# All tiles at set offsets: matmul weights at odd, streamed operands at even multiples of 64 bytes of a partition

## The chip, the core and the metric

The kernel runs on one core of a Trainium2 chip. A core has TensorE (PE), which multiplies; VectorE (DVE), ScalarE (ACT) and GpSimd (POOL), which work on tiles; and SyncE (SP), whose queue issues the DMAs here. On-chip memory (SBUF) has 128 partitions; a tile takes the same range of bytes in each. A matmul on PE is two instructions: a weight load (LDWEIGHTS, shown as PEld), which reads the stationary operand, up to 128 columns, and a MATMUL, which streams the moving operand, up to 512 columns, past it. The weights of the next matmul are loaded while the present one streams, so both operands are read from SBUF at the same time. The metric is the device time of one execution in microseconds; lower is better.

## What is computed

```python
for i in range(2):                  # layer 0: pooling mixer, layer 1: attention
    sh1, sc1, g1, sh2, sc2, g2 = split(silu(c) @ ada_w[i] + ada_b[i], 6)
    a = rms_norm(h, norm_g[i, 0]) * (1 + sc1) + sh1
    h = h + g1 * (pool_mix(a) if i == 0 else attn_mix(a))
    m = rms_norm(h, norm_g[i, 1]) * (1 + sc2) + sh2
    h = h + g2 * (square(relu(m @ mlp_w1[i])) @ mlp_w2[i])   # 1024 -> 4096 -> 1024
return rms_norm(h, final_g)
```

There are 512 latent tokens and 256 context tokens of 1024 channels; the context goes through layer 0 and gives keys and values in layer 1. All of it is in float32.

## The kernel before

**How matmuls are written.** Channels lie on partitions, eight blocks of 128; tokens lie along the free axis. Nearly every operand x is held as two float32r halves, hi and lo with hi + lo = x (helper `hilo`, L91 on ACT and L92 on DVE), and a product is three matmuls: hi·hi, hi·lo, lo·hi. `pe.matmul(out, weights, moving)`: in the profile, `aux<-act,w` is a matmul into PSUM tile aux, with act streamed and w as weights.

**The stages, in order.** Start, pooling mixer and modulation vectors (to about 140 us; L192, L597, L641, L668, L764). The MLP of layer 0 (to about 630 us): 16 chunks of 256 hidden channels each; the first product is L376 in the first chunks and later L444, seven block products in place of eight (`m1_strassen`), with L464 for the context; the second product is L495 (`m2_chunk`), whose results L353 adds to `h_lat` and `h_ctx`. Attention (to about 890 us): L889 projects to keys, values and queries (`project`; here the activations `a_m_hi`, `a_m_lo`, `a_c` are the weights, and the weight tiles `w` are streamed), L967 and L968 are the scores (q as weights, k streamed), L988 transposes, L998 is probabilities by values (v as weights, `act` streamed), L1009 the output product. Then the MLP of layer 1, as in layer 0 but for 512 tokens alone.

**Where the tiles lie.** Pools take SBUF one behind the other in the order in which they are opened, and a pool's slots are its tile size times its number of buffers: `const`, `big` (`act`, `h_lat`, `h_ctx`, `m_hi`, `m_lo`), `wp` (four slots of 8192 bytes, tag `w`), `rp`, `sc`, `sm`, `mc` (five slots of 4096), `raws`, and then the pools of a stage, of which only one set is open at a time: `praws` and `pp` at first; `xs`, `op`, `pair` in the MLP of layer 0; `kvp` (k and v) in attention; `ss`, `fin`, `xs` in the MLP of layer 1. The tiles of `const` begin at a multiple of 128 bytes and take 2976 bytes, 23 times 128 and 32. The small tiles of `sm` take 2112 bytes, 16 times 128 and 64. Everything else that a matmul of float32r reads is a multiple of 128 bytes long. So, of the start of a tile's bytes modulo 128:

| tiles | before |
|---|---|
| `act`, `h_lat`, `h_ctx`, `m_hi`, `m_lo` (all `big`), `w`, `r`, `sc` | 32 |
| `mc` and all in its slots (`m_c`, `a_c`, q, o), `raw`, `xs`, `op`, `pair`, `ada`, k, v | 96 |
| `ident`, `ones` (in `const`) | 0 |

The order of the instructions is the tile framework's (by hand on PE, and for a stretch on DVE and ACT, in the pooling stage). In layer 1 the seven weight sums of a block product take five slots of `mc` and two halves of a tile `spare` in the slot of `h_ctx`:

```python
    def strassen1(m):
        def op():
            spare = new(big, [P, 2, 2, 512], F32R, "h_ctx")
            return lambda n: new(mc, [P, 2, 512], F32R, "mc") if n < 5 else spare[:, n - 5]
```

Of the kernel before, what the change touches and what calls it, by code (L numbers as in the profile page):

```python
# [8 lines left out]
F32 = mybir.dt.float32  # L9
F32R = mybir.dt.float32r  # L10
# [4 lines left out]
P = 128  # L15
D = 1024
KT = D // P
SEQ = 512
CTX = 256
# [4 lines left out]
HD = 128  # L24
# [23 lines left out]
def dit_block_kernel(ctx: ExitStack, tc: tile.TileContext, xT, cols, adab, adaw, w1, w2, wqkv, wo,  # L48
# [4 lines left out]
    def sb(stack, name, bufs):  # L53
        return stack.enter_context(tc.tile_pool(name=name, bufs=bufs))

    const = sb(ctx, "const", 1)
    big = sb(ctx, "big", 1)
    wp = sb(ctx, "wp", 4)
    rp = sb(ctx, "rp", 2)
    sc = sb(ctx, "sc", 4)  # L60
    sm = sb(ctx, "sm", 4)
    mc = sb(ctx, "mc", 5)
# [4 lines left out]
    scope = ExitStack()  # L67
# [2 lines left out]
    accp, rbp = (mc, "mc"), (rp, "r")  # L70

    acts2 = big.tile([P, 2, 4 * T], F32R, tag="act", name="act")
    uid = [0, 0]

    def new(p, shape, dt, tag, bufs=None):
        uid[0] += 1
        kw = {"bufs": bufs} if bufs else {}
        return p.tile(shape, dt, tag=tag, name=f"{tag}{uid[0]}", **kw)
# [17 lines left out]
    nc.sync.dma_start(ident, eye)  # L96
    pcol = const.tile([P, 8, KT], F32, tag="pcol", name="pcol")
    nc.sync.dma_start(pcol, cols)
    h_lat = big.tile([P, KT, SEQ], F32, tag="h_lat", name="h_lat")
    h_ctx = big.tile([P, KT, CTX], F32, tag="h_ctx", name="h_ctx")  # L100
    praw = (praws, [P, 1024], F32, "praw")
    ada_acc = ada_r = None
    edges = pp.tile([P, 4, 2, PAD], F32, tag="edges", name="edges")
# [13 lines left out]
    for u in range(0, 4, 2):  # L117
        pair = new(wp, [P, 2, 1024], F32, "w")
# [271 lines left out]
    def strassen_inputs(m, xs, tmp, cuts):  # L390


        def quarter(i, j):
            return [m[0][x][:, 4 * i : 4 * i + 4, 256 * j : 256 * j + 256] for x in range(2)]

        def total(dst, a, b, op):
            s, e = (new(tmp[0], [P, 4, 256], F32, tmp[1]) for _ in range(2))

            with tc.high_priority(offset=-BEHIND):
                for o, x in ((s, 0), (e, 1)):  # L400
                    dve.tensor_tensor(o, a[x].bitcast(F32), b[x].bitcast(F32), op=op)
                dve.tensor_tensor(s, s, e, op=ALU.add)
                hilo(dst[0], dst[1], s)

        b11, b12, b21, b22 = (quarter(i, j) for i in range(2) for j in range(2))
        b7, b6, b1 = ([t[:, x] for x in range(2)] for t in xs)
        sums = ((b7, b21, b22, ALU.add), (b6, b11, b12, ALU.add), (b1, b11, b22, ALU.add),
                (b12, b12, b22, ALU.subtract), (b21, b21, b11, ALU.subtract))

        def steps(todo):  # L410
            for x in todo:
                total(*x)
                yield
        return (b22, b12, b21, b11, b7, b6, b1), [steps(sums[i:j]) for i, j in zip((0,) + cuts, cuts + (5,))]
# [177 lines left out]
    for k in range(0, KT, 2):  # L592
# [10 lines left out]
        if k % 4 == 2:  # L603
            for i in range(6):
                x = (turned[0][:, i] if i < 4 else turned[1][:, i - 4])[:, k * P - 256 : k * P + 256]
# [239 lines left out]
    def strassen0(m):  # L845
        nonlocal scope, praw, ada_acc, ada_r
        scope.close()
        scope = ExitStack()
        xsp, opp, rawp = sb(scope, "xs", 1), sb(scope, "op", 3), sb(scope, "pair", 1)
        xs = [xsp.tile([P, 2, 4, 256], F32R, tag=f"xs{i}", name=f"xs0{i}") for i in range(3)]  # L850
        praw = (raws, [P, 1024], F32, "raw")
        ada_acc = new(mc, [P, 2, 512], F32, "mc")
        ada_r = [xsp.tile([P, 512], F32R, tag=f"ada{x}", name=f"ada{x}") for x in range(2)]

        def op():
            got = {}

            def tile_of(n):
                for key, pair in (("a", (1, 2)), ("b", (7, 8))):
                    if n in pair:  # L860
                        if key not in got:
                            got[key] = new(wp, [P, 2, 2, 512], F32R, "w")
                        return got[key][:, n - pair[0]]
                return new(opp, [P, 2, 512], F32R, "op")
            return tile_of
        return STRASSEN_FROM[0], strassen_inputs(m, xs, (opp, "op"), (0, 1, 3)), lambda: new(rawp, [P, 2, 1024], F32, "pair"), op

    norm = mlp(0, m, T, last, between=between0, strassen=strassen0, acts=[act0], ws=ws, ahead=lambda: kws.extend(load_w(wqkv[u]) for u in range(2)))
    am_ = lazy_m("a", True)


    scope.close()
    scope = ExitStack()
    kvp = sb(scope, "kvp", 1)
    accp = rbp = (mc, "mc")
    kk = kvp.tile([P, 2, NKV, T], F32R, tag="k", name="k")
    v = kvp.tile([P, 2, 6, NKV * HD], F32R, tag="v", name="v")

    tabs = big.tile([P, 4, 4, HD], F32, tag="h_ctx", name="tabs")
    scale = HD ** -0.5  # L880

    def project(ws, ps, width, tt):
# [228 lines left out]
    scope = ExitStack()  # L1111
# [3 lines left out]
    xsp = sb(scope, "xs", 1)  # L1115

    def strassen1(m):
        def op():
            spare = new(big, [P, 2, 2, 512], F32R, "h_ctx")
            return lambda n: new(mc, [P, 2, 512], F32R, "mc") if n < 5 else spare[:, n - 5]  # L1120

        xs = [xsp.tile([P, 2, 4, 256], F32R, tag=f"xs{i}", name=f"xs{i}") for i in range(3)]
        return STRASSEN_FROM[1], strassen_inputs(m, xs, (mc, "mc"), (1, 3)), lambda: new(fin, [P, 2, 1024], F32, "fin"), op
# [96 lines left out]
```

## Time and profile before

| | us |
|---|---|
| median of 3 runs | 1250.93 (1249.8 to 1253.14) |
| the profiled execution | 1251.34 |
| its span, first to last instruction | 1249.2 |
| PE busy | 1222.6, 7896 matmuls |
| weight loads busy | 1080.2 |
| DVE busy | 1016.9 |
| ACT busy | 589.5 |

The span is what the profile covers; 2.1 us of the execution's time lie around it. PE's busy time is the union of its records, and the record of a matmul is longer than its share of the stream, since one starts before the one ahead of it has ended: the distance from start to start has to be worked out.

### The profile page before, as it was taken

To read this page: it belongs to the slowest core of one execution; us is meant where nothing else is said; L and a number is where in the kernel's file an instruction comes from. 1 tells how busy PE (TensorE), PEld (TensorE's weight loads), DVE (VectorE), ACT (ScalarE), POOL (GpSimd) and SP (SyncE) were. 2 spreads that over 40 slices of the span, in tenths; PEclk is the share of its full clock that TensorE was granted. 3 is DMA by queue.
4 is the path that set the end of the run, shared out by engine and by line. 5 is a ranking of instruction groups with operands and counts; after the bars stand their busy time and mean duration, and the time that the engine had idled before them with its cause. 6 is when DMAs were issued, how large, how long until landed. Compare 5 with 4: busy or idle time off the path is not lost.

```text
span 1249.2 us, 20001 instructions
## 1 busy us (share of the span) xinstructions
PE 1222.6 (98%) x7896; PEld 1080.2 (86%) x7896; DVE 1016.9 (81%) x1723; ACT 589.5 (47%) x1055; POOL 143.1 (11%) x129
## 2 busy tenths in 40 slices
PE   7999999999999999999999999999999999999996
PEld 4767888899999999999988888888988999999996
DVE  6564998888989788866888387879899989898986
ACT  6554533444444444334455264554565454545443
POOL 0300000122131322231012001000000000000002
PEclk9999999999999999999999999999999999999998
DMA  9866424333433333321122020211223332323201
GB/s 351 329 238 218 136 85 139 114 119 119 153 111 133 129 123 120 129 68 34 46 82 85 17 85 18 68 34 67 102 86 101 111 109 92 111 94 110 75 28 68
DMA packets 41310, 138.64 MB, mean 111 GB/s; under 512 B 4736, under 2 KB 8064, under 8 KB 41088
## 3 DMA queue, kind: packets, MB, share of 16 engines
q1 hardware_dynamic: 41216, 137.36, 32.0%
q8 instruction: 62, 1.02, 0.3%
q14 instruction: 32, 0.26, 0.1%
HBM read 135.25 MB, written 2.10 MB: 110 GB/s over the span
## 4 chain that ended last, share of the span: by engine, by line
PE 63%; issue 27%; DVE 4%; ACT 2%; DMA 2%; POOL 1%; SPq 0%; POOLq 0%; DVEq 0%; ACTq 0%
PE aux L495 10%; PE mm L495 10%; PE aux L889 7%; PE mm L444 5%; PE aux L464 5%; PE mm L376 5%; PE aux L444 4%; PE aux L1009 3%; PE aux L998 3%; PE mm L967 2%; DMA raw<-in_dram 2%; PE aux L192 1%; PE mm L668 1%; PE mm L764 1%; PE aux L988 1%
## 5 line engine op out<-in xcount | busy, mean ns | idle before, releaser
L495 PE MATMUL aux<-act,w 128*128 128x512 f32 (+1 forms) x1224 | 238.8, 346 | 0.3 <-DVE h_lat L353 0.2
L495 PE MATMUL mm<-act,w 128*128 128x512 f32 (+1 forms) x1224 | 237.2, 345 | 0.9 <-DVE h_lat L353 0.9
L495 PEld LDWEIGHTS mm<-act,w 128*128 128x128 f32 x1224 | 194.9, 189 | 31.6 <-DVE h_lat L353 1.1
L495 PEld LDWEIGHTS aux<-act,w 128*128 128x128 f32 x1224 | 194.7, 189 | 29.6 <-DVE h_lat L353 0.7
L92 DVE TENSOR_TENSOR w<-raw,w 128x1024 fp32r<-128x1024 f32 x106 | 129.3, 1224 | 28.4 <-ACT w L91 28.3
L91 ACT ACTIVATE w<-raw 128x1024 fp32r<-128x1024 f32 x106 | 110.2, 1056 | 77.6 <-PE aux L495 40.7
L353 DVE SCALAR_TENSOR_TENSOR h_lat<-aux,mod,h_lat 128x512 f32<-128x512 f32 (+1 forms) x180 | 122.4, 686 | 16.9 <-PE aux L495 14.2
L433 POOL TENSOR_TENSOR sc<-pair 128x512 f32<-128x512 f32 x55 | 80.0, 1462 | 314.2 <-DMA raw<-in_dram 106.7
L353 DVE SCALAR_TENSOR_TENSOR h_lat<-mm,mod,h_lat 128x512 f32<-128x512 f32 (+1 forms) x140 | 97.7, 700 | 5.5 <-PE mm L495 4.6
L376 PE MATMUL mm<-m_m_hi,w 128*128 128x512 f32 (+1 forms) x320 | 92.9, 352 | 0.2 <-ACT m_m_hi L91 0.2
L889 PE MATMUL aux<-w,a_m_hi 128*128 128x256 f32 (+1 forms) x384 | 86.3, 320 | 0.0
L224 DVE SCALAR_TENSOR_TENSOR mc<-raw,s_f,mc 128x512 f32<-128x512 f32 x112 | 83.7, 765 | 2.1 <-DMA raw<-in_dram 1.3
L444 PE MATMUL mm<-m_m_hi,mc 128*128 128x256 f32 x384 | 69.8, 281 | 0.0
L889 PEld LDWEIGHTS aux<-w,a_m_hi 128*128 128x128 f32 x384 | 63.4, 190 | 5.0
L376 PEld LDWEIGHTS mm<-m_m_hi,w 128*128 128x128 f32 x320 | 56.3, 189 | 10.2 <-ACT r L384 0.8
L464 PE MATMUL aux<-m_c,w 128*128 128x256 f32 x528 | 61.6, 276 | 0.0
L889 PE MATMUL aux<-w,a_m_lo 128*128 128x256 f32 (+1 forms) x192 | 61.2, 319 | 0.0
L464 PEld LDWEIGHTS aux<-m_c,w 128*128 128x128 f32 x528 | 60.8, 188 | 0.0
L444 PEld LDWEIGHTS mm<-m_m_hi,mc 128*128 128x128 f32 x384 | 59.4, 188 | 0.5
L291 POOL TENSOR_TENSOR sm<-sm,neghalf 128x2 f32<-128x2 f32 (+1 forms) x9 | 6.6, 738 | 443.4 <-DVE sm L289 443.4
L376 PE MATMUL mm<-m_m_lo,w 128*128 128x512 f32 (+1 forms) x160 | 56.1, 351 | 0.7 <-DVE m_m_lo L92 0.7
L444 PE MATMUL mm<-m_m_lo,mc 128*128 128x256 f32 x192 | 53.9, 281 | 0.0
(260 smaller groups left out, 2453.9 us busy)
## 6 DMA issues: line engine op xcount, KB each, us to landing
raw<-in_dram SPq DMA_DIRECT2D x155, 512.0 KB, 3.8
praw<-in_dram SPq DMA_DIRECT2D x34, 512.0 KB, 7.7
fin<-in_dram SPq DMA_DIRECT2D x24, 512.0 KB, 4.4
pair<-in_dram SPq DMA_DIRECT2D x22, 512.0 KB, 4.6
block<-in_dram SPq DMA_DIRECT2D x8, 512.0 KB, 7.2
h_lat<-in_dram SPq DMA_DIRECT2D x4, 512.0 KB, 6.3
w<-in_dram SPq DMA_DIRECT2D x4, 512.0 KB, 10.7
out_dram<-fin SPq DMA_DIRECT2D x8, 256.0 KB, 2.5
```

The source lines that it names most:

```text
L91: act.activation(hi, src, AF.Copy)
L92: lo_eng.tensor_tensor(lo, src, hi.bitcast(F32), op=ALU.subtract)
L224: dve.scalar_tensor_tensor(acc[:, s], w, scal, acc[:, s], op0=ALU.mult, op1=ALU.add)
L353: dve.scalar_tensor_tensor(h, ps, gate[:, dt, s : s + 1], h, op0=ALU.mult, op1=ALU.add)
L376: pe.matmul(ps[:, c0 : c0 + cn], lhs, ms(m, ax, k, c0, cn), start=k + wx + ax == 0, stop=k == KT - 1 and wx == 1)
L433: eng.tensor_tensor(t, x, y, op=how)
L444: pe.matmul(places[n], w[:, wx, k * P : k * P + P], inputs[n][ax][:, k], start=k + wx + ax == 0, stop=k == 3 and wx == 1)
L464: pe.matmul(pc[:, t * 256 : t * 256 + 256], ws[k // 4][:, wx, k % 4 * P : k % 4 * P + P], ms(m, ax, k, SEQ, CTX), start=k + wx + ax == 0, ...
L495: pe.matmul(ps, lhs, a[:, t, ax, c0 : c0 + n], start=t + wx + ax == 0, stop=t == 1 and wx == 1)
L889: pe.matmul(ps, lhs, ws[u][:, wx, o : o + width], start=k + ax + wx == 0, stop=k == KT - 1 and ax == 1)
L998: pe.matmul(po, v[:, vx, k, g * HD : g * HD + HD], pT[:, px, k, j0:j1].rearrange("p j q -> p (j q)"), start=k + vx + px == 0, stop=k == 5 ...
L1009: pe.matmul(ps, ws[j][:, wx, dt * P : dt * P + P], o[ax][:, j, c0 : c0 + n], start=j + wx + ax == 0, stop=j == 1 and ax == 1)
```

## The change

No instruction is added or removed, and none of them changes its shape. Five tiles of spare words, which nothing reads or writes, are put between the pools (`skip`: 8 words of 4 bytes behind `const`, 16 words at the other places), `h_lat`, `h_ctx` and what follows in the slot of `h_ctx` move to a pool of their own, `odd`, and each tile of weight sums in layer 1 takes 1056 words of an `mc` slot and begins 16 words into it, so that all five slots of `mc` are 4224 bytes long.

```diff
     const = sb(ctx, "const", 1)
+    def skip(stack, n=16):
+        uid[2] += 1
+        sb(stack, f"skip{uid[2]}", 1).tile([P, n], F32, tag="skip", name=f"skip{uid[2]}")
+    uid = [0, 0, 0]
+    skip(ctx, 8)
+    odd = sb(ctx, "odd", 1)
+    skip(ctx)
     big = sb(ctx, "big", 1)
+    skip(ctx)
     wp = sb(ctx, "wp", 4)
...
-    h_lat = big.tile([P, KT, SEQ], F32, tag="h_lat", name="h_lat")
-    h_ctx = big.tile([P, KT, CTX], F32, tag="h_ctx", name="h_ctx")
+    h_lat = odd.tile([P, KT, SEQ], F32, tag="h_lat", name="h_lat")
+    h_ctx = odd.tile([P, KT, CTX], F32, tag="h_ctx", name="h_ctx")
...
-        xsp, opp, rawp = sb(scope, "xs", 1), sb(scope, "op", 3), sb(scope, "pair", 1)
+        xsp = sb(scope, "xs", 1)
+        skip(scope)
+        opp, rawp = sb(scope, "op", 3), sb(scope, "pair", 1)
...
+    skip(scope)
     kvp = sb(scope, "kvp", 1)
...
-    tabs = big.tile([P, 4, 4, HD], F32, tag="h_ctx", name="tabs")
+    tabs = odd.tile([P, 4, 4, HD], F32, tag="h_ctx", name="tabs")
...
-            spare = new(big, [P, 2, 2, 512], F32R, "h_ctx")
-            return lambda n: new(mc, [P, 2, 512], F32R, "mc") if n < 5 else spare[:, n - 5]
+            spare = new(odd, [P, 2, 2, 512], F32R, "h_ctx")
+            return lambda n: (new(mc, [P, 1056], F32R, "mc")[:, 16:1040].rearrange("p (x n) -> p x n", x=2) if n < 5
+                              else spare[:, n - 5])
```

By the same sums as before, modulo 128: `h_lat`, `h_ctx`, `w`, `r`, `sc`, `op`, k, v and the weight sums of layer 1 begin at 64; `act`, `m_hi`, `m_lo`, `mc` (with `m_c`, `a_c`, q and o), `raw`, `xs` and `ada` at 0. In the projections (L889) and the scores (L967, L968) the streamed tile is the odd one and the weights are the even one; in every other product of float32r but L232 (both at 0) it is the other way round.

More of the change, by code (lines that the diff above doesn't have):

```diff
@@ L72, in dit_block_kernel @@
     acts2 = big.tile([P, 2, 4 * T], F32R, tag="act", name="act")
-    uid = [0, 0]
     def new(p, shape, dt, tag, bufs=None):
```

## The prediction

> **What bounds the kernel now.** I read the page first, then busy time by stages of 50 us, who PE waits for, the groups of matmuls by form, and the timeline of PE alone.
>
> ```profile
> span 1249.2 us, 20001 instructions
> ...
> PE 1222.6 (98%) x7896; PEld 1080.2 (86%) x7896; DVE 1016.9 (81%) x1723; ACT 589.5 (47%) x1055; POOL 143.1 (11%) x129
> ...
> PEclk9999999999999999999999999999999999999998
> ```
>
> PE is busy nearly throughout, at full granted clock. Its waits for others are small, and the largest two are these, of the order of 9 us together, at the start and at the scores:
>
> ```profile
> PE mm L597 <- DMA h_lat<-in_dram: 6.8, 2, 6.3
> PE mm L967 <- ACT mc L91: 2.0, 4, 0.5
> ```
>
> So the time is set by how fast PE takes matmul after matmul. The share of busy time doesn't tell that, since records overlap. The timeline does, where one form follows itself: the run's length less one record, divided by the count less one, is the distance from start to start.
>
> ```profile
> 251.32 4.47 PE L444 MATMUL aux<-xs,op 128*128 128x256 f32 x36
> 255.64 5.60 PE L464 MATMUL aux<-m_c,w 128*128 128x256 f32 x48
> ```
>
> Both runs have 256 columns and 128 columns of weights. With the mean record of the first table below, L464 goes at (5600 - 276) / 47 = 113.3 ns and L444 at (4470 - 283) / 35 = 119.6 ns. Nothing is waited for in either. What differs is the place in SBUF: in L464 the streamed `m_c` begins at 96 modulo 128 bytes and the weights at 32; in L444 `xs` and `op` both begin at 96. In both rows record less distance is 163 ns, so the mean record of a form tells its distance: 276 stands for 113.3, 283 for 120. For 512 columns the same holds:
>
> ```profile
> 701.70 10.89 PE aux L889 x48
> ```
>
> Here 48 matmuls of 512 columns start within 10.89 us, 226.9 ns each, twice 113.3 within the reading; a record of 226.7 + 163 = 389.7 is the undisturbed one. Now the twenty largest forms (line, tiles out<-streamed,weights, count, busy us, mean record in ns):
>
> ```profile
> L495 PE MATMUL mm<-act,w 128*128 128x512 f32 x696 | 206.8, 393 | 0.0
> L495 PE MATMUL aux<-act,w 128*128 128x512 f32 x696 | 204.1, 394 | 0.3 <-DVE h_lat L353 0.2
> L495 PE MATMUL mm<-act,w 128*128 128x256 f32 x528 | 119.8, 281 | 0.9 <-DVE h_lat L353 0.9
> L495 PE MATMUL aux<-act,w 128*128 128x256 f32 x528 | 114.3, 281 | 0.0
> L444 PE MATMUL mm<-m_m_hi,mc 128*128 128x256 f32 x384 | 69.8, 281 | 0.0
> L376 PE MATMUL mm<-m_m_hi,w 128*128 128x512 f32 x192 | 68.5, 396 | 0.0
> L464 PE MATMUL aux<-m_c,w 128*128 128x256 f32 x528 | 61.6, 276 | 0.0
> L444 PE MATMUL mm<-m_m_lo,mc 128*128 128x256 f32 x192 | 53.9, 281 | 0.0
> L376 PE MATMUL mm<-m_c,w 128*128 128x256 f32 x192 | 53.4, 278 | 0.0
> L444 PE MATMUL aux<-xs,op 128*128 128x256 f32 x396 | 50.0, 283 | 0.0
> L889 PE MATMUL aux<-w,a_m_hi 128*128 128x256 f32 x256 | 46.5, 283 | 0.0
> L889 PE MATMUL aux<-w,a_m_hi 128*128 128x512 f32 x128 | 39.8, 392 | 0.0
> L376 PE MATMUL mm<-m_m_lo,w 128*128 128x512 f32 x96 | 37.8, 393 | 0.0
> L967 PE MATMUL mm<-k,mc 128*128 128x512 f32 x96 | 37.2, 420 | 2.2 <-ACT mc L91 2.0
> L889 PE MATMUL aux<-w,a_m_lo 128*128 128x256 f32 x128 | 36.2, 283 | 0.0
> L444 PE MATMUL aux<-xs,h_ctx 128*128 128x256 f32 x288 | 35.9, 279 | 0.0
> L1009 PE MATMUL aux<-mc,w 128*128 128x512 f32 x144 | 35.2, 392 | 0.0
> L444 PE MATMUL mm<-m_m_hi,op 128*128 128x256 f32 x176 | 34.7, 281 | 0.0
> L444 PE MATMUL mm<-m_m_hi,w 128*128 128x256 f32 x176 | 33.6, 283 | 0.0
> L998 PE MATMUL aux<-act,v 128*128 128x512 f32 x126 | 30.6, 395 | 0.0
> ```
>
> No form of 256 columns is under 276 and none of 512 is under 390. The distances look like steps: 113.3, 120 and 226.7 ns are 17, 18 and 34 times 6.67 ns. If a step is the time of 16 columns, which are 64 bytes of float32, then a matmul beside a weight load loses between nothing and one line of 64 bytes. I read this as two readers meeting in one half of the memory, the half being chosen by the 64-byte bit of the address. It is a reading, and the rivals start from other ones.
>
> **The change, part by part.** It leaves the instructions, their order and their shapes alone. The skipped words cost bytes and no time, as nothing touches them. What moves is the offset at which PE's two operands begin, and that of every other engine and DMA.
>
> *The loss that is there to win.* For the rows of 256 columns, count times (record - 276): L495 2 x 528 x 5 = 5.28 us; L444 with `mc` 384 x 5 + 192 x 5 = 2.88; with `xs,op` 396 x 7 = 2.77; with `xs,h_ctx` 288 x 3 = 0.86; `m_hi,op` 176 x 5 = 0.88; `m_hi,w` 176 x 7 = 1.23; L376 `m_c` 192 x 2 = 0.38; L889 384 x 7 = 2.69. Sum 16.97 us. For 512, against 389.7: L495 696 x 3.3 + 696 x 4.3 = 5.29; L376 192 x 6.3 + 96 x 3.3 = 1.53; L889 128 x 2.3 = 0.29; L1009 144 x 2.3 = 0.33; L998 126 x 5.3 = 0.67. Sum 8.11 us. L967 is left out, as its 420 ns hold waits. Together 25.1 us in 5946 matmuls, 2% of the time, and this is all that the meeting of readers costs in these rows.
>
> *What the change does to it.* After it, weights lie at 64 and streamed tiles at 0 in all these rows but L889. That is the layout of L464 (streamed 96, weights 32) moved on by 32 bytes. If the layout gives what it gives in L464, 528 times over, 25.1 - 2.98 (L889) = 22.1 us go. The other end: two other rows have L464's offsets already, L376 with `m_c` (278) and L444 with `xs,h_ctx` (279), and over the three the loss is (192 x 2 + 288 x 3) / 1008 = 1.24 ns; L1009, with the same offsets and 512 columns, loses 2.3. With these, the 2380 matmuls of 256 columns that now have another layout go from 13.04 to 2.95 us, and the 1806 of 512 (L495, L376, L998) from 7.49 to 4.15: 13.4 us are won. I take 22.1, since L464 is the largest of these rows and the only one that never leaves 276, and since starts at 64 and 0 split no 64-byte line between two halves, as starts at 32 and 96 do.
>
> *L889 and the scores* stand the other way round, streamed at 64 and weights at 0. The nearest row is L444 with `mc` (streamed 32, weights 96): 281. L889 would go from 283 to 281 in 384 matmuls, 0.8 us at best; at 512 columns the nearest is L998 (streamed 32, weights 96),
>
> ```profile
> 732.07 4.36 PE L998 MATMUL aux<-act,v 128*128 128x512 f32 x18
> ```
>
> (4360 - 395) / 17 = 233.2 ns (35 steps), 6.5 over 226.7, where L889 now loses 2.3: 128 x 4.2 = 0.5 us lost. I put the two at nothing.
>
> *The other engines.* DVE, ACT, POOL and the DMAs do the same work at new offsets. No row shows them at 0 or 64, so I bound them by what would reach PE. DVE is closest to it (stretch and length, then busy us with the count for PE, weight loads, DVE, ACT and POOL):
>
> ```profile
> 150.00:200.00 50.00, 50.00 (x289) 43.34 (x288) 48.67 (x65) 18.78 (x23) 1.30 (x1) 1.00 0.29 95
> ...
> 900.00:950.00 50.00, 50.00 (x297) 44.41 (x296) 47.38 (x62) 25.48 (x39) 0.70 (x1) 1.00 0.32 98
> 950.00:1000.00 50.00, 50.00 (x281) 43.85 (x281) 47.74 (x63) 25.24 (x36) 0.00 (x0) 1.00 0.34 114
> ```
>
> DVE's slack is 1.3 us of 50 in the first of these and 2.3 to 2.6 in the others. A PE that is 22.1 / 1249 = 1.8% faster asks for 0.9 us per 50, so DVE stays behind PE, just. Were DVE's operations 3% slower at the new offsets, these stages would need 50.1, 48.8 and 49.2 us where PE needs 49.1, and lose 1.0, 0 and 0.1 us: I take nothing, and up to 2 us as the worse end. A faster DMA or DVE wins nothing, as only the 9 us of waits could shrink. The wider slots of `mc` hold the same tiles and set free no one earlier or later.
>
> *Sum.* 1251.3 us of the profiled execution less 22.1 is 1229.2. That execution lies 0.4 above the median of the runs, so against the median 1229.
>
> **Rivals.** *The grid itself matters (B).* Even the best rows may pay for starting at 32 or 96: 113.3 ns are 17 steps, where 256 columns of 4 bytes have 16 lines of 64, and 226.7 are 34, where 512 columns have 32. Started on a line, a matmul could take fewer. PE can go faster than 113.3:
>
> ```profile
> 736.26 0.82 PE L988 MATMUL aux<-ident,r 128*128 128x128 f32 x6
> ```
>
> ```profile
> L988 PE MATMUL aux<-ident,r 128*128 128x128 f32 x192 | 26.4, 273 | 0.4 <-DVE r L978 0.4
> ```
>
> Six transposes, (820 - 273) / 5 = 109 ns apart (0.82 us less one mean record of 273, over five). At 109 and 218 the rows gain a further 3772 x 4.3 + 2174 x 8.7 = 35.1 us and L889 its 3: 1251.3 - 25.1 - 35.1 = 1191. The far end is set by the weight load, whose record grows from 108 to 188 ns between 32 and 128 columns:
>
> ```profile
> L464 PEld LDWEIGHTS aux<-m_c,w 128*128 128x128 f32 x528 | 60.8, 188 | 0.0
> ...
> L192 PEld LDWEIGHTS aux<-praw,s_w 128*32 128x32 f32 x136 | 4.1, 108 | 10.9 <-issue 7.2 <-DMA praw<-in_dram 3.5
> ```
>
> That is 0.83 ns a column, 106.7 for 128: 3772 x 6.6 + 2174 x 13.3 = 53.8 more than the 25.1, and 1172. Against it: a whole line lost at 256 and two at 512 look like a rate, which may belong to float32r and not to the start; and at 5% DVE's slack above would be used up. [...]
>
> *The offsets don't decide (C).* `xs,h_ctx` has L464's offsets and runs at 279, L495, with both operands at 32, is at 281 and not at 283, and the 48 matmuls of L889 above, both at 32 too, lose nothing. Then the loss comes from how the two streams fall into step, which a shift doesn't mend: what L464 wins or loses, L495 gives back, and the time stays within 0.3%, 1247.6 to 1255.1, about what a measurement of this kernel can tell from no change. [...]
>
> *Aligned lines meet (D, slower).* Both streams now change lines at the same instants, and while one line of weights is read, two of the moving operand pass, one in each half. So wherever the weights begin, each load could meet the stream and cost one line, 6.7 ns. That decides if even one such meeting per load is unavoidable on the grid, which the split lines of now sometimes escape. All rows at 283 and 396.4: 3772 x 7 - 16.97 = 9.4 us, and 2174 x 6.7 - 8.11 = 6.5 us; 1251.3 + 15.9 = 1267. For it: `mc` and v as weights at 96, the half that is nominally odd, are at 281 and 395, worse than `w` at 32. Against it: no row but `xs,op`, `m_hi,w` and L889, all with equal offsets, is at 283.
>
> **How the numbers follow.** The forecast (A, 1229, between 1229 and 1238) has 0.42, B 0.25, C 0.17, D 0.16. The range goes from 1177, which takes in B but for its far end, to 1254, which takes in C; D is left out, and the rest of B. Faster by over 0.3% are A and B, 0.67; within 0.3% is C, 0.17; slower is D, 0.16.
>
> **What would show it.** The counts must stay: 7896 matmuls and as many loads. By A, L464 stays at 276, and `xs,op`, `m_hi,w`, L495 and L444 with `mc` come down to 276 and 390; L889 stays at about 283. By B, L464 itself and the rows of 512 fall under 276 and 389. By D, L464 rises to 283. By C, rows move both ways and the sum doesn't. In the stages from 900 to 1000 us DVE should come to 97%; if PE then shows waits for DVE there, the gain is cut by them. The forecast is wrong if L495, which has 10.6 of the 25.1 us, keeps 281 and 393.

## The result, and the profile after

The changed kernel takes 1254.94 us (median of 12 executions, 1252.67 to 1257.23), the kernel before 1251.77. The ratio is 1.0024, with a 95% interval of 1.0015 to 1.0033: slower by 0.24%, or 3.2 us. The profiled execution took 1254.41 us.

The page of the kernel after, its span and the busy time by engine:

```profile
span 1252.3 us, 20001 instructions
...
PE 1225.7 (98%) x7896; PEld 1077.9 (86%) x7896; DVE 1019.5 (81%) x1723; ACT 588.2 (47%) x1055; POOL 140.8 (11%) x129
...
PEclk9999999999999999999999999999999999999999
```

As many instructions as before, the same clock, and 3.1 us more span, all of it in PE's busy time. Who PE waits for (us in total, times, longest), in the kernel after:

```profile
PE mm L607 <- DMA h_lat<-in_dram: 6.8, 2, 6.4
PE mm L980 <- ACT mc L101: 2.0, 4, 0.5
```

The same 6.8 and 2.0 us. So neither an engine nor a transfer came between: the matmuls themselves follow each other more slowly. The groups of matmuls by form show which (L505 was L495, L454 was L444, L474 L464, L386 L376, L902 L889):

```profile
L505 PE MATMUL mm<-act,w 128*128 128x512 f32 x696 | 209.3, 396 | 0.0
L505 PE MATMUL aux<-act,w 128*128 128x512 f32 x696 | 207.0, 398 | 0.2
L505 PE MATMUL mm<-act,w 128*128 128x256 f32 x528 | 119.2, 280 | 1.1 <-DVE h_lat L363 1.1
...
L454 PE MATMUL mm<-m_m_hi,mc 128*128 128x256 f32 x384 | 69.7, 280 | 0.0
L386 PE MATMUL mm<-m_m_hi,w 128*128 128x512 f32 x192 | 69.1, 398 | 0.0
L474 PE MATMUL aux<-m_c,w 128*128 128x256 f32 x528 | 63.9, 280 | 0.0
...
L902 PE MATMUL aux<-w,a_m_hi 128*128 128x256 f32 x256 | 45.5, 280 | 0.0
...
L454 PE MATMUL aux<-xs,h_ctx 128*128 128x256 f32 x288 | 34.6, 276 | 0.0
```

The rows of 512 columns rose: those of L505 from 393 and 394 to 396 and 398 (696 x 3 + 696 x 4 = 4.9 us), that of L386 from 396 to 398. L474 rose from 276 to 280 (528 x 4 = 2.1 us), `m_c` in L386 from 278 to 281. Most of the other rows of 256 columns fell, by 1 to 4 ns, and `xs,mc` from 283 to 276. The second product of layer 1 shows the rise at 512 columns best. PE's timeline, first one row of before, then four of after (start, length in us):

```profile
984.45 2.91 PE L495 MATMUL mm<-act,w 128*128 128x512 f32 x12
```

```profile
252.63 4.40 PE L454 MATMUL aux<-xs,op 128*128 128x256 f32 x36
256.87 5.77 PE L474 MATMUL aux<-m_c,w 128*128 128x256 f32 x48
...
984.97 2.88 PE L454 MATMUL aux<-xs,h_ctx 128*128 128x256 f32 x24
987.69 2.96 PE L505 MATMUL mm<-act,w 128*128 128x512 f32 x12
```

Before: (2910 - 393) / 11 = 228.8 ns; after: (2960 - 396) / 11 = 233.1. And L474 goes at (5770 - 280) / 47 = 116.8 instead of 113.3, while `xs,op` goes at 117.7 instead of 119.6 and `xs,h_ctx` at 113.2.

In what follows a **distance in bytes** is the start of the weights less the start of the streamed operand beside which they are loaded, modulo 256. The change moved it so: `act,w` and `m,w` from 0 to 64, `m_c,w` from 192 to 64 and 192 in turn (the `mc` slots of 4224 bytes alternate by 128), `xs,op` from 0 to 64, `m,mc` from 64 to 64 and 192, L889's `w,a_m` from 0 to 192; `xs,h_ctx` stayed at 192 and `act,v` at 64.

**Lost time** below is the sum, over all matmuls of float32r that another one follows, of the time from start to start less 113.3 ns (256 columns) or 226.7 (512). Single steps that are over 25 ns too long hold waits and stops and are left out. It is 29.3 us before and 31.9 after, 2.6 of the 3.1 us by which the span grew.

### The profile page after: what moved, and what is told of

It is laid out like the page before. It is cut to its first block, busy times and chain, and to the rows that moved or that the text cites. A ratio compares the mean times of both kernels' runs of the same rounds, so it can differ in the third digit from the quotient of the medians.

```text
span 1252.3 us, 20001 instructions
## 1 busy us (share of the span) xinstructions
PE 1225.7 (98%) x7896; PEld 1077.9 (86%) x7896; DVE 1019.5 (81%) x1723; ACT 588.2 (47%) x1055; POOL 140.8 (11%) x129
## 4 chain that ended last, share of the span: by engine, by line
PE 63%; issue 27%; DMA 3%; DVE 3%; ACT 2%; POOL 1%; SPq 0%; POOLq 0%; DVEq 0%; ACTq 0%
PE aux L505 10%; PE mm L505 10%; PE aux L902 8%; PE aux L474 5%; PE mm L454 5%; PE mm L386 5%; PE aux L454 4%; PE aux L1022 3%; PE aux L1011 3%; PE mm L980 2%; DMA raw<-in_dram 2%; PE mm L774 1%; PE aux L1001 1%; PE mm L678 1%; PE aux L202 1%
## 5 line engine op out<-in xcount | busy, mean ns | idle before, releaser
L505 PE MATMUL aux<-act,w 128*128 128x512 f32 (+1 forms) x1224 | 240.7, 347 | 0.2
L505 PE MATMUL mm<-act,w 128*128 128x512 f32 (+1 forms) x1224 | 238.7, 346 | 1.1 <-DVE h_lat L363 1.1
L505 PEld LDWEIGHTS mm<-act,w 128*128 128x128 f32 x1224 | 194.3, 188 | 33.8 <-DVE h_lat L363 1.3
L505 PEld LDWEIGHTS aux<-act,w 128*128 128x128 f32 x1224 | 194.1, 188 | 32.1 <-DVE h_lat L363 0.6
L386 PE MATMUL mm<-m_m_hi,w 128*128 128x512 f32 (+1 forms) x320 | 93.2, 353 | 0.3 <-ACT m_m_hi L101 0.2
L902 PE MATMUL aux<-w,a_m_hi 128*128 128x256 f32 (+1 forms) x384 | 85.5, 318 | 0.0
L454 PE MATMUL mm<-m_m_hi,mc 128*128 128x256 f32 x384 | 69.7, 280 | 0.0
L902 PEld LDWEIGHTS aux<-w,a_m_hi 128*128 128x128 f32 x384 | 62.7, 188 | 5.1
L386 PEld LDWEIGHTS mm<-m_m_hi,w 128*128 128x128 f32 x320 | 56.0, 188 | 11.0 <-ACT r L394 0.8
L474 PE MATMUL aux<-m_c,w 128*128 128x256 f32 x528 | 63.9, 280 | 0.0
L474 PEld LDWEIGHTS aux<-m_c,w 128*128 128x128 f32 x528 | 62.9, 188 | 0.0
L902 PE MATMUL aux<-w,a_m_lo 128*128 128x256 f32 (+1 forms) x192 | 60.8, 317 | 0.0
L454 PEld LDWEIGHTS mm<-m_m_hi,mc 128*128 128x128 f32 x384 | 59.6, 188 | 0.5
L386 PE MATMUL mm<-m_m_lo,w 128*128 128x512 f32 (+1 forms) x160 | 56.2, 352 | 0.7 <-DVE m_m_lo L102 0.7
L386 PE MATMUL mm<-m_c,w 128*128 128x256 f32 x192 | 53.9, 281 | 0.0
```

The source lines that it names most:

```text
L386: pe.matmul(ps[:, c0 : c0 + cn], lhs, ms(m, ax, k, c0, cn), start=k + wx + ax == 0, stop=k == KT - 1 and wx == 1)
L454: pe.matmul(places[n], w[:, wx, k * P : k * P + P], inputs[n][ax][:, k], start=k + wx + ax == 0, stop=k == 3 and wx == 1)
L474: pe.matmul(pc[:, t * 256 : t * 256 + 256], ws[k // 4][:, wx, k % 4 * P : k % 4 * P + P], ms(m, ax, k, SEQ, CTX), start=k + wx + ax == 0, ...
L505: pe.matmul(ps, lhs, a[:, t, ax, c0 : c0 + n], start=t + wx + ax == 0, stop=t == 1 and wx == 1)
L902: pe.matmul(ps, lhs, ws[u][:, wx, o : o + width], start=k + ax + wx == 0, stop=k == KT - 1 and ax == 1)
```

## The experiments

The theories at first were these. 1: the relative place of weights and streamed operand decides, and the width of the matmul decides which place is good. 2: the 64-byte grid itself costs or gains. 3: the offsets decide nothing, and how two streams fall into step is chance.

**Matmuls alone.** A kernel that leaves out all the rest streams tiles `ma` to `md`, starting at 0, 32, 64 and 96 modulo 128, past weights `wa` to `wd` that start alike. By the sizes of the tiles, pairs of the same letter are at distance 0 modulo 256 too, `ma,wc` and `mb,wd` at 64.

> The matmuls alone: runs of 48 float32r matmuls of zeros, in the order hi-hi, hi-lo, lo-hi, with the streamed tile starting at 0, 32, 64 or 96 bytes modulo 128 (ma, mb, mc, md) and the weights likewise (wa, wb, wc, wd), 512 and 256 columns wide, each once behind a pause of transposes and once chained; the rest of the computation is left out and the output is zero. Theory 1 (only whether both begin in the same 64-byte half counts, and the width decides which is better): at 512 columns the pairs aa, ab, ba, bb and cc, cd, dc, dd go at 226.7 ns and the others at 233 to 235; at 256 the same pairs go at 120 and the others at 117.7 or 113.3; starts at 0 and 32 do not differ. Theory 2 (starts on the 64-byte grid cost, split lines escape): bb and bd at 512 and db, bd at 256 are faster than aa, ac, ca by 4 ns or more. Theory 3 (chance of the phase, nothing in the offsets): the same pair gives different distances behind the pause and chained, and no pair is better on average by over 1 ns.

Groups by form, with one run of 48 matmuls in a row:

```profile
L87 PE MATMUL chained<-ma,wc 128*128 128x512 f32 x48 | 11.4, 394 | 0.0
...
L87 PE MATMUL chained<-ma,wb 128*128 128x512 f32 x48 | 11.4, 395 | 0.0
...
L87 PE MATMUL chained<-ma,wa 128*128 128x512 f32 x48 | 11.1, 390 | 0.0
...
L87 PE MATMUL chained<-mc,wc 128*128 128x512 f32 x48 | 11.1, 389 | 0.0
...
L87 PE MATMUL chained<-mb,wb 128*128 128x256 f32 x48 | 5.9, 282 | 0.0
...
L87 PE MATMUL chained<-mb,wd 128*128 128x256 f32 x48 | 5.6, 276 | 0.0
```

Equal starts are the best for 512 columns, on the grid of 32 or on that of 64, and among the worst for 256, where 64 apart gives 276. Theory 2 has nothing here. Theory 1 has its first miss: `ma,wb`, with both starts in the same half, was to go at 226.7 ns and goes at 233 by the starts in the trace. Of theory 3, one part holds at 256 columns: by the starts, `mc,wa` goes at 117.8 ns behind a pause and at 113.3 chained. The other part falls: at 512 columns equal letters are the best both ways, by 2 ns and more (but for the very first run, whose records have 442 ns on average).

**The grid in the whole kernel**, from both sides: the changed kernel without its first eight spare words (weights at 32, streamed operands at 96), and the kernel before with eight words behind `const`.

```diff
-    skip(ctx, 8)
```

> The changed kernel without its first 8 spare words: weights at 32 and streamed tiles at 96 everywhere, so the halves stay different and the grid of the kernel before comes back; this is what L464 had before, for all products. Theory 1 (halves): as the changed kernel, 1254.9 us, the 512-column rows of the second product at 396 to 398 ns. Theory 2 (grid): the loss of the 512-column rows is gone, 390 ns, and with the 256-column rows at 276 to 280 the time is 1229 to 1247. Theory 3: within 0.1% of either kernel.

```diff
     const = sb(ctx, "const", 1)
+    sb(ctx, "skip", 1).tile([P, 8], F32, tag="skip", name="skip")
```

> The kernel before with 8 spare words behind the constants and nothing else: every tile moves by 32 bytes, onto the 64-byte grid, and all pairs keep their relation. Theory 1 (halves): as the kernel before, 1251.8 us, the 512-column rows of the second product at 393 and those of layer 1 at 390. Theory 2 (grid): 1255 or more, the 512-column rows at 396 to 398. Theory 3: within 0.1% of either kernel.

The first took 1254.34 us, ratio 1.0021 (1.0011 to 1.0031), the second 1251.41, ratio 1.0000 (0.9990 to 1.0009), both against 1251.48. Off the grid the changed kernel stays slow, on it the old one stays as it was. What does it is the place of the tiles to each other.

**`act` moved to an odd place in the changed kernel**, so that it lies with the weights modulo 128; modulo 256 it is then 128 away from them.

```diff
-    acts2 = big.tile([P, 2, 4 * T], F32R, tag="act", name="act")
+    acts2 = odd.tile([P, 2, 4 * T], F32R, tag="act", name="act")
```

> The changed kernel with the act tile moved into the pool of the odd tiles, so that the second product of both MLPs has streamed tile and weights in the same half again, and all else stays as changed. Theory 1 (halves by width): its 512-column rows come back to 393 and 390 ns (4.4 us), the 256-column matmuls between 512-column ones win 1.2 us, the ones behind one another lose 2.1 us: 1254.9 - 3.5 = 1251.4. Theory 2 (grid): no change from 1254.9. Theory 3: within 0.1% of either.

1250.03 us, ratio 0.9984 (0.9976 to 0.9993): within 1.4 us of the total that was expected, but not by its rows:

```profile
L505 PE MATMUL mm<-act,w 128*128 128x512 f32 x696 | 208.7, 394 | 0.1
L505 PE MATMUL aux<-act,w 128*128 128x512 f32 x696 | 206.3, 396 | 0.3
L505 PE MATMUL mm<-act,w 128*128 128x256 f32 x528 | 120.6, 283 | 0.8 <-DVE h_lat L363 0.8
...
L454 PE MATMUL mm<-m_m_hi,mc 128*128 128x256 f32 x384 | 68.0, 277 | 0.0
```

The rows of 512 columns win back about half of their loss and not all of it (the runs of twelve in layer 1 still go at 233.7 ns by their starts), 256 columns are worse, and the gain came in the first product, which the edit doesn't touch (280 to 277). Theory 1 had the modulus wrong.

**The modulus, in steps of 32 bytes.** Again matmuls alone: one stream `m`, weights `wa` to `wq` at 0 to 512 bytes behind it, runs of 36; then other widths, and a first matmul of another width ahead.

> The matmuls alone again, with zeros, the rest of the computation left out and the output zero: one streamed tile, and weights at 0, 32, ... 512 bytes behind it modulo 512 (wa, wb, ... wq), 36 matmuls each, behind a pause and chained, at 512 and 256 columns; then 512 and 256 in turn, other widths, and a first matmul of another width ahead of the run. The kernel with act among the odd tiles had streams and weights both at 64 modulo 128 and yet lost 6.5 ns at 512 columns; its distance was 128. Theory 1 (distance of weights behind the stream modulo 256 decides, by width): 512 columns: 226.7 ns at 0 and 256 and 512, 228.9 at 192 and 448, 233 at 64, 128 and 320; 256 columns: 120 at 0, 128, 256, 113.3 or 117.8 at 64 and 192. Theory 2 (no memory of the distance beyond the half, the loss is inherited from the products around): 128 behaves as 0, 226.7 at 512 columns and 120 at 256. Which of 113.3 and 117.8 comes depends on the width of the first matmul if the phase of entry decides.

PE's timeline, for 0 (`wa`), 64 (`wc`), 128 (`we`), 192 (`wg`) and 256 bytes (`wi`), first with 256 columns, then with 512:

```profile
258.13 4.48 PE L87 MATMUL chained<-m,wa 128*128 128x256 f32 x36
270.89 4.43 PE L87 MATMUL chained<-m,we 128*128 128x256 f32 x36
283.70 4.47 PE L87 MATMUL chained<-m,wi 128*128 128x256 f32 x36
300.80 4.26 PE L87 MATMUL chained<-m,wc 128*128 128x256 f32 x36
313.47 4.25 PE L87 MATMUL chained<-m,wg 128*128 128x256 f32 x36
330.33 8.36 PE L87 MATMUL chained<-m,wa 128*128 128x512 f32 x36
355.17 8.53 PE L87 MATMUL chained<-m,we 128*128 128x512 f32 x36
380.35 8.33 PE L87 MATMUL chained<-m,wi 128*128 128x512 f32 x36
413.72 8.56 PE L87 MATMUL chained<-m,wc 128*128 128x512 f32 x36
438.69 8.41 PE L87 MATMUL chained<-m,wg 128*128 128x512 f32 x36
```

The period is 256: `wi` is like `wa`, `we` is not, and behind a pause all pairs 256 bytes apart agree within 0.2 ns. At 512 columns 0 is the best ((8330 - 389) / 35 = 226.9 ns), 192 the next (229.1), 64 the worst of these (233.3). At 256 columns it is the reverse: 0 is the worst (119.9), 64 and 192 the best (113.8 and 113.5). But, by the starts in the trace, 192 goes at 117.8 ns with a pause ahead of the run; and at 64 a first matmul of 128 columns leads to 113.3, one of 160 columns to 117.8 (past the first eight matmuls of a run):

```profile
619.87 2.96 PE L87 MATMUL lead<-m,wc 128*128 128x256 f32 x24
...
626.48 3.03 PE L87 MATMUL lead<-m,wc 128*128 128x256 f32 x24
```

So 64 and 192 have two ways to go, and **what stands ahead of the run decides which**. At 192 all eight widths that were tried ahead, 128 to 240, led to 117.8; only a run chained to others went at 113.3.

**`act` alone moved by 64 in the kernel before.**

```diff
+    sb(ctx, "skipa", 1).tile([P, 16], F32, tag="skipa", name="skipa")
+    apart = sb(ctx, "apart", 1)
+    acts2 = apart.tile([P, 2, 4 * T], F32R, tag="act", name="act")
+    sb(ctx, "skipb", 1).tile([P, 16], F32, tag="skipb", name="skipb")
     big = sb(ctx, "big", 1)
...
-    acts2 = big.tile([P, 2, 4 * T], F32R, tag="act", name="act")
```

> The kernel before with act alone moved by 64 bytes against all else (16 words ahead of it and behind it): one part of the change alone. Theory 1: the second product goes from distance 0 to 64, its 512-column rows from 393 to 397 (4.2 us lost), its 256-column matmuls between 512-column ones lose 1.2 us, the ones behind one another win 2.2: before + 3.2 = 1254.9. Theory 2 (inherited from the first product's layout): 1251.5 as before, rows unchanged.

1251.63 against 1251.71 us, ratio 1.0005 (0.9996 to 1.0014). By the total theory 1 is wrong; the groups tell more:

```profile
L499 PE MATMUL mm<-act,w 128*128 128x512 f32 x696 | 209.2, 396 | 0.0
L499 PE MATMUL aux<-act,w 128*128 128x512 f32 x696 | 207.0, 398 | 0.3 <-DVE h_lat L357 0.2
...
L448 PE MATMUL mm<-m_m_hi,mc 128*128 128x256 f32 x384 | 67.4, 276 | 0.0
...
L448 PE MATMUL aux<-xs,h_ctx 128*128 128x256 f32 x288 | 34.6, 276 | 0.0
```

The second product lost just what it lost in the changed kernel. `m,mc` and `xs,h_ctx`, whose distances are untouched, won 384 x 5 + 192 x 5 + 288 x 3 = 3.7 us (the middle term is `m_m_lo,mc`, also 281 to 276). The reading is that they come behind a second product that now ends in another phase.

**The changed kernel, with `act` at distance 0 again**: `act` has a pool of its own behind the third `skip`, directly ahead of `wp`.

```diff
     skip(ctx)
+    apart = sb(ctx, "apart", 1)
     wp = sb(ctx, "wp", 4)
...
-    acts2 = big.tile([P, 2, 4 * T], F32R, tag="act", name="act")
+    acts2 = apart.tile([P, 2, 4 * T], F32R, tag="act", name="act")
```

> The changed kernel with act moved behind the third spare tile, directly ahead of the weight pool: same bytes, all pairs as changed, but act and w at distance 0 modulo 256, as in the kernel before. Theory 1: the 512-column rows of the second product come back to 393 and 390 (4.2 us), those of probabilities by values too (0.8 us), 256 columns: 1.2 us won and 2.3 lost: 1254.9 - 3.9 = 1251.0, or less if the first product keeps the better phase that it had in the run with act among the odd tiles (another 5 us, 1246). Theory 2: 396 to 398 stay, 1254.9.

1246.15 against 1251.71 us, ratio 0.9961 (0.9948 to 0.9974): this one beats both kernels.

```profile
L506 PE MATMUL mm<-act,w 128*128 128x512 f32 x696 | 206.6, 393 | 0.2 <-DVE act L399 0.2
L506 PE MATMUL aux<-act,w 128*128 128x512 f32 x696 | 203.9, 394 | 0.3 <-DVE h_lat L364 0.3
...
L387 PE MATMUL mm<-m_m_hi,w 128*128 128x512 f32 x192 | 69.2, 398 | 0.0
L475 PE MATMUL aux<-m_c,w 128*128 128x256 f32 x528 | 63.1, 278 | 0.0
...
L455 PE MATMUL aux<-xs,op 128*128 128x256 f32 x396 | 48.2, 278 | 0.4 <-POOL op L103 0.4
```

The 512 columns are back at 393 and 394, and `xs,op` went on to 278 (283 before, 282 in the changed kernel). Lost time is 23.7 us, 5.6 less than before, and the measured medians differ by 5.6. That the two agree so closely is partly chance: in the profiled executions the single steps left out of the lost time grew by 1.5 us, and the time outside the float32r products shrank by about as much.

**The first product's tiles alone moved, in the kernel before**: `xs` and `h_ctx` by 64 bytes, and v to distance 0, by words in front and behind.

```diff
...
+    skip(ctx, 16)
+    hc = sb(ctx, "hc", 1)
+    skip(ctx, 48)
...
-    h_ctx = big.tile([P, KT, CTX], F32, tag="h_ctx", name="h_ctx")
+    h_ctx = hc.tile([P, KT, CTX], F32, tag="h_ctx", name="h_ctx")
...
-        xsp, opp, rawp = sb(scope, "xs", 1), sb(scope, "op", 3), sb(scope, "pair", 1)
+        skip(scope, 48)
+        xsp = sb(scope, "xs", 1)
+        skip(scope, 16)
+        opp, rawp = sb(scope, "op", 3), sb(scope, "pair", 1)
...
+    skip(scope, 48)
+    vp = sb(scope, "vp", 1)
...
+    skip(scope, 48)
     fin = sb(scope, "fin", 2)
...
```

> The kernel before with xs, h_ctx and v alone moved by 64 bytes (each by 16 or 48 skipped words, the words behind them filled up to 256 bytes, so that everything else keeps its distance): weights behind xs by 64 instead of 0 (op, mc) and 192 (h_ctx), v behind act by 0 instead of 64. Theory that stands (the distance modulo 256 bytes decides, with the width): xs,op goes from 283 to about 278 (396 x 5 = 2.0 us), xs,h_ctx from 279 to 276 (288 x 3 = 0.9), act,v from 395 to 392 (126 x 3 = 0.4), the second product keeps 393 and 394 at 512 columns, m_hi,w keeps 283: 1251.6 - 3.3 = 1248.3, if m_c,w keeps its 276. That row tells two causes apart: if it lost in the changed kernel because its distance alternates there between 64 and 192, it stays at 276 here, where it is 192 throughout; if it takes its phase from the xs,op before it, it rises to 278 or more and gives 1.1 to 1.4 us back, 1249.5. Rival (offsets don't decide, the rows only trade with each other): 1251.6.

1251.01 against 1251.47 us, ratio 0.9994 (0.9986 to 1.0003): most of the expected 3.3 us didn't come, and the total alone fits the rival, by which rows only trade with each other. The rows tell more:

```profile
L469 PE MATMUL aux<-m_c,w 128*128 128x256 f32 x528 | 63.6, 279 | 0.0
...
L449 PE MATMUL aux<-xs,op 128*128 128x256 f32 x396 | 49.3, 281 | 0.0
...
L449 PE MATMUL aux<-xs,h_ctx 128*128 128x256 f32 x288 | 35.9, 281 | 0.0
...
L1008 PE MATMUL aux<-act,v 128*128 128x512 f32 x126 | 30.0, 391 | 0.0
```

At 512 columns the distance held to the rule (395 to 391). At 256 columns `xs,op` and `xs,h_ctx` have the good distance of 64 and go the slower way, 281, which stands for 118. And `m_c,w`, at 192 throughout as before, rose from 276 to 279: it takes its phase from the `xs,op` ahead of it, and the alternation of 64 and 192 isn't needed for that. Two of the eleven runs of `m_c,w` show it within this one kernel:

```profile
290.86 5.82 PE L469 MATMUL aux<-m_c,w 128*128 128x256 f32 x48
...
324.30 5.61 PE L469 MATMUL aux<-m_c,w 128*128 128x256 f32 x48
```

That is (5820 - 279) / 47 = 117.9 ns and (5610 - 279) / 47 = 113.4. By the starts, `xs,op` ahead of the second run goes at 117.8, stops once (two steps of 150 and 222 ns), goes on at 113.3, and `m_c,w` keeps that; the run at 392.32 us is alike. Ahead of the other nine `xs,op` doesn't stop, and all nine go at 117.8 or 117.9.

## Why the prediction was wrong

**The step that failed** is "If the layout gives what it gives in L464, 528 times over, 25.1 - 2.98 (L889) = 22.1 us go", and with it the other end of 13.4. It carried the offsets of one row of 256 columns to rows of 512, where the runs show them to be among the worst: 64 apart costs 233.3 ns where 0 gives 226.9. Two halves told apart by the 64-byte bit, as the prediction read its steps, no run shows: at 128 bytes, which is the same half as 0, 512 columns go at (8530 - 395) / 35 = 232.4 ns. L495 and L376 had the best distance already and lost it. The only row of 512 columns that was used as a bound, L1009, has a distance of 192, which is the mild case (229.1); modulo 128 it looks the same as 64. The evidence stood in the trace before: the twelve matmuls of L495 above at 228.8 ns, and the 48 of L889 at 226.9 ns that rival C names, have equal offsets and lose nearly nothing, while `act,v`, at 64 apart, had 395.

**L464 itself** didn't stay at 276 as case A asked. Its 276 was a phase that it got from the product ahead of it, as the last experiment shows (279 on average at the same distance of 192, and 113.4 or 117.9 ns by run), and no property of its layout alone. The rows with `xs,h_ctx` (279) and `m_c` in L376 (278), taken for the cautious end, were the warning. Two slips came with it. The 22.1 us include the losses of `xs,h_ctx`, of `m_c` in L376 and of L1009 (0.86 + 0.38 + 0.33 us), which had that layout already, so that on the prediction's own reading the change had nothing to win there. And the count of 5946 matmuls takes in the 96 of L967 that the sum leaves out.

**The rest of the sum.** L889 was put at 281 in place of 283 and came to 280 and 279; its 512 columns were put at a loss of 0.5 us and lost 128 x 1 = 0.1. DVE got hardly slower at the new offsets: 1019.5 us busy for the same 1723 instructions, where it had 1016.9. The three stages that bounded it:

```profile
150.00:200.00 50.00, 50.00 (x287) 43.15 (x286) 48.49 (x64) 19.08 (x24) 1.29 (x1) 1.00 0.29 96
900.00:950.00 50.00, 49.88 (x302) 43.58 (x301) 46.95 (x62) 27.52 (x42) 0.70 (x1) 1.00 0.29 95
950.00:1000.00 50.00, 50.00 (x264) 42.23 (x263) 47.28 (x63) 24.23 (x35) 0.00 (x0) 1.00 0.29 95
```

48.5, 47.0 and 47.3 us of DVE where it had 48.7, 47.4 and 47.7. The size of what there was to win was about right (25.1 us by rounded records, 29.3 by starts), but the losses outweighed the gains: by starts, L505 at 512 columns lost 4.2 us, L474 2.3, L386 (512 columns and `m_c`) 1.2, and all other rows together won 5.0.

**The rivals.** B (the grid) fell: 1.0000 with the old kernel on the grid, and at 256 and 512 columns no float32r run came to its 109 and 218 ns: the best are 113.3 and 226.7. C gave a range that holds the result (to 1255.1; the forecast's range, said to take C in, stopped at 1254), and its reading, that the loss comes from how two streams fall into step, fits one part of what the runs show: at 256 columns and 64 or 192 bytes the same pair goes at 113.3 or 117.8 ns, by what stands ahead. But that a shift can't mend it is refuted by 1246.15 us; and with the matmuls alone, behind the same pause, 36 of 512 columns take 8.44 us with the weights at distance 0 and 8.65 at 64. D's 396.4 at 512 columns did come (396 and 398), its 283 at 256 did not (280 in L505). A loss at every load, wherever the weights begin, is not what the runs show: with the matmuls alone 512 columns go at 226.9 ns at distance 0, and 256 at 113.8 and 113.5 at 64 and 192.

**What stays open.** The loss isn't a sum over products, since a product at distance 64 or 192 with 256 columns can keep the pace at which it begins, as `m_c,w` did at 113.4 or 117.9 ns in the last experiment: `act` alone moved gives nothing, the first product alone nothing, all but `act` gives 5.6 us, everything loses 3.2. What sets the phase at a change of product, and why the period is 256 bytes, no run here tells. The lost time is also not the whole time: for the kernel with `act` at an odd place it fell by 3.6 us and the span of the profiled execution by only 1.8, mainly since the single steps left out of it, the waits and stops, grew by 1.5 us (14.3 to 15.8). Why these grew is not shown.

## What to carry to other kernels

Where PE runs without a gap, work out for each product the start of the weights less the start of the streamed operand modulo 256 bytes. For float32r with 128 columns of weights loaded for each matmul, which is all that was measured here, ask for 0 at 512 columns (226.9 ns, where 64 gave 233.3) and for 64 or 192 at 256 (113.8 and 113.5 chained, where 0 gave 119.9); one rule for all tiles isn't enough. A good distance is judged in the whole kernel and not product by product, since a run of 256 columns at 64 or 192 went at 113.3 or at 117.8 ns by what stood ahead of it. A figure read from one group is carried over only to groups of the same width, and a layout is compared modulo more than one candidate period.

## What the runs showed of the hardware

All paces here are by the starts in the trace of the matmuls alone in steps of 32 bytes, past the first eight matmuls of a run, float32r with its own weight load for each. The best were 173.3 ns at 384 columns and 226.7 at 512, which is 53.4 ns for 128 columns more. As an estimate from these two, 226.7 - 4 x 53.4 = 13.1 ns don't grow with the width. The 119.9 ns of 256 columns at distance 0 fit this too (2 x 53.4 + 13.1 = 119.9), and the 146.7 of 320 (2.5 x 53.4 + 13.1 = 146.6); at 64 or 192, in the runs that go at 113.3, only 113.3 - 106.8 = 6.5 ns are left beside the columns. By this estimate the 17 steps for 256 columns and 34 for 512, which the prediction read as a possible rate, are better read as 16 + 1 and 32 + 2.

Which distance is best changed with the width. 320 columns go at 146.7 ns at 0, 64, 128 and 192 alike (24 matmuls take 3.76 or 3.77 us), 384 at 173.3 at 0 and 192 (4.42 and 4.41 us, and 4.49 and 4.45 at 64 and 128), 448 at 200.0 at 192 and at 202.7 at 0 (5.06 and 5.11 us).

From 128 to 240 columns the pace hardly depended on the width:

```profile
513.11 2.88 PE L87 MATMUL width<-m,wa 128*128 128x128 f32 x24
...
537.88 2.93 PE L87 MATMUL width<-m,wa 128*128 128x240 f32 x24
```

24 matmuls of 128 columns take 2.88 us and 24 of 240 columns 2.93, or 111.6 and 112.0 ns each. What sets this pace is not shown.
